# A binary cross-entropy over 8192 x 8192: seven small loads moved between the first large ones, and the last three stores dealt out anew

## The chip, the core and the metric

The kernel runs on one core of a Trainium2 chip. The metric is device time in microseconds (us), lower is better. The kernel before takes 1867.31 us as the median of three runs (1867.1 to 1867.54).

## The reference

Both inputs are 8192 x 8192 float32, 268 MB each, and so is the output.

```python
pred = np.clip(pred, eps, 1 - eps)          # eps = 1e-7
return -(target * np.log(pred) + (1 - target) * np.log(1 - pred))
```

`target` holds only 0 and 1, so every output element is the negative logarithm of either `pred` or `1 - pred`. Nothing is reduced: each element is read once from each input and written once.

## The kernel before, in words

The 67.1 million elements are laid over 128 partitions, 524,288 elements to each. `plan` cuts these into 37 chunks: two of 7680 columns (chunks 0 and 1), 32 of 15,360 columns (chunks 2 to 33), two of 7680 (chunks 34 and 35), and a last one of 2048 columns (chunk 36). All of it lives in two ring tiles, `ring_p` in float32 (the prediction, overwritten in place by every step up to the result) and `ring_t` in bfloat16 (the target, converted by the load itself). Each ring has two slots of 15,360 columns, which are used in turn, and a place of its own for chunk 36. A chunk of the small size takes half a slot.

One chunk goes through these steps. `load` brings target and prediction (L70, L71). `front_of` clips the prediction on VectorE (L100), adds `target - 1` on VectorE (L103), and takes the absolute value and the logarithm on ScalarE (L106, L107): |p + t - 1| is p where t is 1 and 1 - p where t is 0. `back_of` negates on VectorE (L110). `store` writes the result (L77). Large chunks are worked in two halves of 7680 columns, `(0, 2)` and `(1, 2)`.

The order on each engine is the order of the lines: the schedule is written by hand (`tc.manual_schedule`), and every engine issues its own instructions in that order and waits at each for what it needs. Nearly all DMAs are issued by GpSimd (POOL in the profile). SyncE (SP) issues only the prediction's load of chunk 0 and the stores of the last chunks, here chunks 34 and 35. A load into a slot waits for the store that empties the slot. Each of GpSimd's DMAs signals one of eight semaphores, taken in turn, and so it also waits for the DMA eight places before it on that engine to have landed. The DMA that an engine issues is split over 16 DMA engines, each of which works through its part of one queue in order.

Chunk 36 is loaded and stored in another layout (`mixed`, L81 to L83), and the prediction's part of it in uneven pieces, which the code calls teeth: a piece is 32 partitions by some multiple of 256 columns (`STEP`). One unit of 256 columns over 32 partitions is 32 KB, and the chunk has 32 units. The seven early pieces (`EARLY`, L93) have 8, 6, 4, 2, 6, 4 and 2 units; the eight late pieces (`LATE`, L97), which store the same chunk, have 8, 1, 4, 6, 6, 1, 2 and 4.

At the start the kernel before issues, on GpSimd, the target of chunk 0, target and prediction of chunk 1, target and prediction of chunk 2, and then four early pieces (L120 to L122). The other three early pieces follow the loads of chunk 3 (L132). In the main loop (L133 to L143) chunk k is worked and stored, and the chunk two places on is loaded. At the end (L144 to L158) z is chunk 33 and a and b are chunks 34 and 35: z is stored in two halves, a and b whole. On VectorE both halves of b's front come before the negation of a.

Of the kernel before, what the change touches and what calls it, by code (L numbers as in the profile page):

```python
# [1 line left out]

# [4 lines left out]

EPS = 1e-7

BIG = 15 * 1024  # L10
HALF = BIG // 2
STEP = 256
EARLY = ((0, 0, 8), (1, 0, 6), (2, 0, 4), (3, 0, 2), (3, 2, 8), (2, 4, 8), (1, 6, 8))
LATE = (
    (0, 0, 8), (1, 0, 1), (2, 0, 4), (3, 0, 6),
    (1, 2, 8), (1, 1, 2), (3, 6, 8), (2, 4, 8),
)


def plan(total):  # L20

    n, last = divmod(total, BIG)
    assert n > 4 and 0 < last <= 2048
    spots = [(HALF, 0), (HALF, HALF)]
    spots += [(BIG, k % 2 * BIG) for k in range(1, n - 1)]
    end = (n - 1) % 2 * BIG
    return spots + [(HALF, end), (HALF, end + HALF), (last, 2 * BIG)]

@with_exitstack
def kernel(
    ctx: ExitStack,
    tc: tile.TileContext,
    pred: bass.AP,
    target: bass.AP,
    out: bass.AP,
):
    nc = tc.nc
    fp32 = mybir.dt.float32  # L40
    bf16 = mybir.dt.bfloat16
    Alu = mybir.AluOpType
    Act = mybir.ActivationFunctionType
    P = nc.NUM_PARTITIONS

    R, C = pred.shape
    spots = plan(R * C // P)
    n = len(spots)
    widths = [w for w, _ in spots]
    cols = [sum(widths[:k]) for k in range(n)]  # L50

    def chunk(ap, k):
        flat = ap.rearrange("r c -> (r c)")
        end = R * C - cols[k] * P
        return flat[end - widths[k] * P : end].rearrange("(p w) -> p w", p=P)

    pool = ctx.enter_context(tc.tile_pool(name="rings", bufs=1))
    ring = [P, 2 * BIG + widths[-1]]
    ring_p = pool.tile(ring, fp32, name="ring_p", tag="ring_p")
    ring_t = pool.tile(ring, bf16, name="ring_t", tag="ring_t")  # L60
    warm = pool.tile([1, 8], fp32, name="warm", tag="warm")

    def spot(ring, k, part=(0, 1)):
        w, c = spots[k]
        i, m = part
        return ring[:, c + i * w // m : c + (i + 1) * w // m]

    def load(k):
        queue = nc.sync if k == 0 else nc.gpsimd
        nc.gpsimd.dma_start(out=spot(ring_t, k), in_=chunk(target, k))  # L70
        queue.dma_start(out=spot(ring_p, k), in_=chunk(pred, k))  # L71

    def store(k, part=(0, 1)):
        queue = nc.sync if k >= n - 3 else nc.gpsimd
        i, m = part
        w = widths[k] // m
        queue.dma_start(  # L77
            out=chunk(out, k)[:, i * w : (i + 1) * w], in_=spot(ring_p, k, part)
        )

    def mixed(ap):  # L81
        flat = ap.rearrange("r c -> (r c)")[: widths[-1] * P]
        return flat.rearrange("(b a w) -> a b w", b=8, a=16)  # L83

    def tooth_of(ap, j, lo, hi):
        return mixed(ap)[4 * j : 4 * j + 4, :, lo * STEP : hi * STEP]

    def tooth_in(j, lo, hi):
        return spot(ring_p, n - 1)[32 * j : 32 * j + 32, lo * STEP : hi * STEP]

    def load_teeth(teeth):
        for tooth in teeth:
            nc.gpsimd.dma_start(out=tooth_in(*tooth), in_=tooth_of(pred, *tooth))  # L93

    def store_teeth(teeth):
        for tooth in teeth:
            nc.gpsimd.dma_start(out=tooth_of(out, *tooth), in_=tooth_in(*tooth))  # L97

    def front_of(p, t):
        nc.vector.tensor_scalar(  # L100
            out=p, in0=p, scalar1=EPS, scalar2=1 - EPS, op0=Alu.max, op1=Alu.min
        )
        nc.vector.scalar_tensor_tensor(  # L103
            out=p, in0=t, scalar=1.0, in1=p, op0=Alu.subtract, op1=Alu.add
        )
        nc.scalar.activation(out=p, in_=p, func=Act.Abs)  # L106
        nc.scalar.activation(out=p, in_=p, func=Act.Ln)  # L107

    def back_of(p):
        nc.vector.tensor_scalar(out=p, in0=p, scalar1=-1.0, scalar2=None, op0=Alu.mult)  # L110

    def front(k, *part):
        front_of(spot(ring_p, k, *part), spot(ring_t, k, *part))

    def back(k, *part):
        back_of(spot(ring_p, k, *part))

    with tc.manual_schedule():
        nc.vector.memset(warm, 1.0)  # L119
        for k in range(3):  # L120
            load(k)
        load_teeth(EARLY[:4])  # L122
        nc.scalar.activation(out=warm, in_=warm, func=Act.Ln)  # L123
        front(0)
        front(1)
        back(0)
        store(0)
        back(1)
        store(1)
        load(3)  # L130
        nc.gpsimd.dma_start(out=spot(ring_t, n - 1), in_=mixed(target))  # L131
        load_teeth(EARLY[4:])  # L132
        for k in range(2, n - 4):  # L133
            front(k, (0, 2))
            front(k, (1, 2))
            back(k, (0, 2))
            back(k, (1, 2))
            store(k)
            for j in range(k + 2, n - 1 if k == n - 5 else k + 3):
                load(j)  # L140
            if k == 4:
                front(n - 1)
                back(n - 1)  # L143
        z, a, b = range(n - 4, n - 1)  # L144
        front(z, (0, 2))
        front(z, (1, 2))
        back(z, (0, 2))
        store(z, (0, 2))
        front(a)
        back(z, (1, 2))  # L150
        store(z, (1, 2))
        store_teeth(LATE)
        front(b, (0, 2))
        front(b, (1, 2))
        back(a)
        store(a)
        back(b)
        store(b)  # L158


# [1 line left out]
_INS = ['pred', 'target']  # L162
_OUTS = [((8192, 8192), 'float32')]


# [23 lines left out]
```

## Time and profile before

| | |
|---|---|
| median of three runs | 1867.31 us (1867.1 to 1867.54) |
| the profiled execution, its own time | 1866.22 us |
| its span in the trace | 1864.3 us |
| DMA engines, busy share in each fortieth of the span | 9 tenths or more |
| moved between HBM and the core | 536.87 MB read, 268.44 MB written |
| VectorE busy | 1122.4 us (60%) |
| ScalarE busy | 900.0 us (48%) |
| GpSimd busy | 68.6 us (4%) |

The span begins with the first instruction and ends with the last, and all points in time below count from its start. An engine's busy time leaves out its waits. A DMA is shown by the instruction that issues it and by the time from that to its landing, which is the moment when the last of the 16 DMA engines reports its part. The trace also keeps the report of each single DMA engine, so 16 landing times stand for each transfer; where the text says mean, first or last of the landings, these are meant. The loads of the target count with their bfloat16 size in the rate of the profile (GB/s), which is half of what they read.

### The profile page before, as it was taken

Reading aid. Unit: us, or ns where it says so; the run is one execution under the profiler, and the core shown is the slowest. Engines: PE = TensorE matmul, PEld = TensorE weight load, DVE = VectorE, ACT = ScalarE, POOL = GpSimd, SP = SyncE. Lnnn points to the kernel's source line nnn. Section 1 sums busy time; section 2 is a strip of 40 time slices with the busy share of each in tenths; the row PEclk is TensorE's granted clock in tenths of the full one; section 3 lists DMA queues with packets and bytes.
Section 4 is the critical chain, followed back from the end, with each engine's and each line's share of the span. In section 5 each row is a group of like instructions: output and inputs, shape, how many; then the busy total and the mean of one; then the engine's idle time right before and its main releaser. Section 6 shows DMA issues by size and latency. Waiting matters only on the chain.

```text
span 1864.3 us, 640 instructions
## 1 busy us (share of the span) xinstructions
DVE 1122.4 (60%) x210; ACT 900.0 (48%) x142; POOL 68.6 (4%) x126
## 2 busy tenths in 40 slices
DVE  4646676555666555566665556666555766555585
ACT  3345553345554334555433455543345554334555
POOL 1000000000000000000000000000000000000001
DMA  9999999999999999999999999999999999999999
GB/s 295 370 340 353 344 358 380 387 358 351 353 344 358 381 388 362 347 352 345 357 381 388 363 345 355 344 357 383 384 364 345 352 345 357 384 384 365 345 344 390
DMA packets 17620, 671.14 MB, mean 360 GB/s; under 512 B 3152, under 2 KB 3152, under 8 KB 3600
## 3 DMA queue, kind: packets, MB, share of 16 engines
q0 software_dynamic: 17184, 659.31, 98.7%
q1 hardware_dynamic: 432, 11.80, 1.5%
q14 instruction: 4, 0.03, 0.0%
HBM read 536.87 MB, written 268.44 MB: 432 GB/s over the span
## 4 chain that ended last, share of the span: by engine, by line
DMA 35%; issue 25%; ACT 23%; DVE 15%; POOL 1%; POOLq 0%; DVEq 0%; PEldq 0%
DMA ring_p<-in_pred_dram 32%; ACT ring_p L106 12%; ACT ring_p L107 11%; DVE ring_p L103 7%; DVE ring_p L100 4%; DVE ring_p L110 4%; DMA out_dram<-ring_p 3%; POOL ring_t L70 1%; POOL out_dram L77 0%; POOL ring_p L71 0%; POOLq L77 0%; DVEq L100 0%; POOLq L71 0%; PEldq L184 0%; POOLq L70 0%
## 5 line engine op out<-in xcount | busy, mean ns | idle before, releaser
L106 ACT ACTIVATE ring_p<-ring_p 128x7680 f32<-128x7680 f32 (+2 forms) x70 | 450.6, 6437 | 943.1 <-DVE ring_p L103 943.1
L103 DVE SCALAR_TENSOR_TENSOR ring_p<-ring_t,ring_p 128x7680 f32<-128x7680 bf16 (+2 forms) x70 | 557.2, 7960 | 2.4
L100 DVE TENSOR_SCALAR ring_p<-ring_p 128x7680 f32<-128x7680 f32 (+2 forms) x70 | 284.0, 4058 | 395.9 <-DMA ring_p<-in_pred_dram 395.9
L110 DVE TENSOR_SCALAR ring_p<-ring_p 128x7680 f32<-128x7680 f32 (+1 forms) x69 | 284.1, 4117 | 328.9 <-ACT ring_p L107 328.9
L107 ACT ACTIVATE ring_p<-ring_p 128x7680 f32<-128x7680 f32 (+2 forms) x70 | 451.1, 6444 | 2.2
L71 POOL DMA_DIRECT2D ring_p<-in_pred_dram x35 | 18.7, 534 | 921.7 <-DMA out_dram<-ring_p 921.7
L77 POOL DMA_DIRECT2D out_dram<-ring_p x35 | 19.8, 567 | 824.2 <-DVE ring_p L110 799.2
L70 POOL DMA_DIRECT2D ring_t<-in_target_dram x36 | 19.9, 552 | 1.1 <-PEq L184 0.8
L93 POOL DMA_DIRECT2D ring_p<-in_pred_dram x7 | 5.2, 762 | 16.3 <-DMA ring_t<-in_target_dram 16.3
L97 POOL DMA_DIRECT2D out_dram<-ring_p x8 | 4.7, 594 | 12.4 <-DMA out_dram<-ring_p 12.4
L123 ACT ACT_TABLE_LOAD x1 | 1.3, 1283 | 0.7 <-PEq L173 0.7
L131 POOL DMA_DIRECT2D ring_t<-in_target_dram x1 | 0.6, 557 | 0.0
L119 DVE MEMSET warm<- 1x8 f32 x1 | 0.1, 65 | 0.8 <-PEq L173 0.8
L123 ACT ACTIVATE warm<-warm 1x8 f32<-1x8 f32 x1 | 0.2, 207 | 0.0
L173 POOL MEMSET const-float32-0.0<- 128x1 f32 x1 | 0.1, 98 | 0.2 <-issue 0.2
L173 POOL MEMSET const-bfloat16-1.0<- 128x1 bf16 x1 | 0.1, 101 | 0.0
L173 POOL MEMSET const-float32-1.0<- 128x1 f32 x1 | 0.1, 98 | 0.0
L173 POOL MEMSET const-uint8-127<- 128x1 uint8 x1 | 0.1, 98 | 0.0
## 6 DMA issues: line engine op xcount, KB each, us to landing
ring_p<-in_pred_dram POOLq DMA_DIRECT2D x32, 7680.0 KB, 35.9
out_dram<-ring_p POOLq DMA_DIRECT2D x31, 7680.0 KB, 29.2
ring_t<-in_target_dram POOLq DMA_DIRECT2D x32, 3840.0 KB, 46.8
out_dram<-ring_p POOLq DMA_DIRECT2D x4, 3840.0 KB, 29.9
ring_p<-in_pred_dram POOLq DMA_DIRECT2D x3, 3840.0 KB, 35.0
ring_t<-in_target_dram POOLq DMA_DIRECT2D x4, 1920.0 KB, 27.7
out_dram<-ring_p SPq DMA_DIRECT2D x2, 3840.0 KB, 12.8
ring_p<-in_pred_dram SPq DMA_DIRECT2D x1, 3840.0 KB, 18.8
```

The costliest lines, as they stand in the source:

```text
L70: nc.gpsimd.dma_start(out=spot(ring_t, k), in_=chunk(target, k))
L71: queue.dma_start(out=spot(ring_p, k), in_=chunk(pred, k))
L77: queue.dma_start(out=chunk(out, k)[:, i * w : (i + 1) * w], in_=spot(ring_p, k, part))
L93: nc.gpsimd.dma_start(out=tooth_in(*tooth), in_=tooth_of(pred, *tooth))
L97: nc.gpsimd.dma_start(out=tooth_of(out, *tooth), in_=tooth_in(*tooth))
L100: nc.vector.tensor_scalar(out=p, in0=p, scalar1=EPS, scalar2=1 - EPS, op0=Alu.max, op1=Alu.min)
L103: nc.vector.scalar_tensor_tensor(out=p, in0=t, scalar=1.0, in1=p, op0=Alu.subtract, op1=Alu.add)
L106: nc.scalar.activation(out=p, in_=p, func=Act.Abs)
L107: nc.scalar.activation(out=p, in_=p, func=Act.Ln)
L110: nc.vector.tensor_scalar(out=p, in0=p, scalar1=-1.0, scalar2=None, op0=Alu.mult)
L123: nc.scalar.activation(out=warm, in_=warm, func=Act.Ln)
L131: nc.gpsimd.dma_start(out=spot(ring_t, n - 1), in_=mixed(target))
```

## The change

At the start, the order on GpSimd becomes: targets of chunks 0 and 1, four early pieces, prediction of chunk 1, target of chunk 2, the other three early pieces, prediction of chunk 2. (The prediction of chunk 0 stays on SyncE.) The three pieces behind the loads of chunk 3 are gone from there.

At the end, the second half of z's store goes to SyncE instead of GpSimd. The negation of a and its store come between the two halves of b's front. The negation and the store of b are done in two halves of 3840 columns.

```diff
+    def load_t(k):
+        nc.gpsimd.dma_start(out=spot(ring_t, k), in_=chunk(target, k))
+
+    def load_p(k):
+        queue = nc.sync if k == 0 else nc.gpsimd
+        queue.dma_start(out=spot(ring_p, k), in_=chunk(pred, k))
+
     def load(k):
-        queue = nc.sync if k == 0 else nc.gpsimd
-        nc.gpsimd.dma_start(out=spot(ring_t, k), in_=chunk(target, k))
-        queue.dma_start(out=spot(ring_p, k), in_=chunk(pred, k))
+        load_t(k)
+        load_p(k)
 
     def store(k, part=(0, 1)):
-        queue = nc.sync if k >= n - 3 else nc.gpsimd
         i, m = part
+        queue = nc.sync if k >= n - 3 or (k == n - 4 and i) else nc.gpsimd
...
         nc.vector.memset(warm, 1.0)
-        for k in range(3):
-            load(k)
+        load_p(0)
+        load_t(0)
+        load_t(1)
         load_teeth(EARLY[:4])
+        load_p(1)
+        load_t(2)
+        load_teeth(EARLY[4:])
+        load_p(2)
         nc.scalar.activation(out=warm, in_=warm, func=Act.Ln)
...
         nc.gpsimd.dma_start(out=spot(ring_t, n - 1), in_=mixed(target))
-        load_teeth(EARLY[4:])
...
         store_teeth(LATE)
         front(b, (0, 2))
-        front(b, (1, 2))
         back(a)
         store(a)
-        back(b)
-        store(b)
+        front(b, (1, 2))
+        back(b, (0, 2))
+        store(b, (0, 2))
+        back(b, (1, 2))
+        store(b, (1, 2))
```

## The prediction

> **What bounds the kernel now.** I read the page's slices and queues first, then the waits, then the timeline of the two ends.
>
> From the page, the slices and the traffic:
>
> ```profile
> DMA  9999999999999999999999999999999999999999
> GB/s 295 370 340 353 344 358 380 387 358 351 353 344 358 381 388 362 347 352 345 357 381 388 363 345 355 344 357 383 384 364 345 352 345 357 384 384 365 345 344 390
> HBM read 536.87 MB, written 268.44 MB: 432 GB/s over the span
> ```
>
> The DMA engines are busy from the first slice to the last. The rate swings because target loads are counted at half of what they read; by HBM traffic it is 432 GB/s over the whole span. The chain of work repeats this: the predictions of successive chunks are issued at 1680.37, 1734.73 and 1789.07, so a chunk takes 54.35 us for three transfers (target, prediction, result) that each have 7680 KB on the HBM side. That is 18.12 us for a transfer of 7680 KB and 9.06 us for one of 3840 KB. These two prices carry the rest.
>
> The waits say the same from the engines' side:
>
> ```profile
> ACT ring_p L106 <- DVE ring_p L103: 943.1, 36, 32.1
> POOL ring_p L71 <- DMA out_dram<-ring_p: 921.7, 32, 35.9
> DVE ring_p L100 <- DMA ring_p<-in_pred_dram: 395.9, 36, 18.7
> ```
>
> VectorE and ScalarE wait for data. GpSimd's long wait for a store to land looks like a stall and is none for the DMA engines: while prediction 3 waits until 98.55 for a slot, the target issued at 70.77 is still under way until 116.0 (45.3 us to landing).
>
> The time therefore is the DMA work of the slowest DMA engine plus whatever time it idles at the two ends. The timeline of the last 40 us:
>
> ```profile
> 1800.81 0.54 POOL L77 DMA_DIRECT2D out_dram<-ring_p  x1 [10.15 <-DVE ring_p L110]
> 1825.11 2.16 DVE L100 TENSOR_SCALAR ring_p<-ring_p 128x3840 f32<-128x3840 f32 x1 [1.65 <-DMA ring_p<-in_pred_dram]
> 1826.33 1.07 POOL L77 DMA_DIRECT2D out_dram<-ring_p  x1 [24.98 <-issue]
> 1827.39 3.53 POOL L97 DMA_DIRECT2D out_dram<-ring_p  x6
> 1837.65 4.15 DVE L110 TENSOR_SCALAR ring_p<-ring_p 128x7680 f32<-128x7680 f32 x1
> 1841.83 8.84 SPq L77 DMA_DIRECT2D out_dram<-ring_p  x2
> 1843.89 0.59 POOL L97 DMA_DIRECT2D out_dram<-ring_p  x1 [8.83 <-DMA out_dram<-ring_p]
> 1846.15 4.16 DVE L110 TENSOR_SCALAR ring_p<-ring_p 128x7680 f32<-128x7680 f32 x1 [4.35 <-ACT ring_p L107]
> ```
>
> And the stretches of 5 us, where the last two columns are the DMA share and the rate:
>
> ```profile
> 1830.00:1835.00 5.00, 4.97 (x3) 5.00 (x2) 1.46 (x3) 1.00 1.04 449
> 1835.00:1840.00 5.00, 5.00 (x2) 4.97 (x3) 0.06 (x1) 1.00 0.90 361
> 1840.00:1845.00 5.00, 1.80 (x1) 4.97 (x2) 0.59 (x1) 1.00 0.89 327
> 1845.00:1850.00 5.00, 3.85 (x1) 1.11 (x1) 0.00 (x0) 1.00 1.06 452
> ```
>
> There is the one visible hole: between 1835 and 1845 the rate is 361 and 327 against 432. The missing (71 + 105) GB/s over 5 us each are 0.88 MB, or 2.0 us of the 16 engines' work. What matters is whose it is.
>
> **Who idles at the end.** The landings, by issue plus time to landing, for the last engine: prediction of b 1825.1, first half of z 1834.2 (33.4 us after issue), second half of z 1843.6 (17.3), a 1854.3 (12.5), last late piece 1854.4 (10.5), b 1863.4 (13.1). Between prediction b and the end lie 38.3 us, of which four transfers of 9.06 are 36.2. The other 2.1 are pieces: 0.6 for the 2 of 32 units that fall to it (64 KB over four engines, at the same rate), and 1.5 for completions, since the landings of pieces on engines that get none of their data still come 0.18 apart, and there are eight. So the last engine has no idle time. The first engine is another matter: it reports the second late piece at 1838.89, the seventh at 1841.11 and a at 1852.29, which is 11.2 after the seventh, against 9.06 of work: it idled 2.1 us because a was issued only at 1841.83. The mean of the 16 landings shows 9.9 between them, 0.8 idle. At the end, the mean of the landings of b is 1862.42 and the last 1863.43. The hole is real, but it belongs to engines that finish early anyway.
>
> **The change, start.** Seven pieces, 1 MB, move from behind prediction 2 and behind prediction 3 to places between the first loads. The data are the same and so is the number of transfers, so the work of each DMA engine stays.
>
> - GpSimd's queue: targets 0 and 1, four pieces (about 0.6 us each to issue, from the four at L93), prediction 1, target 2 are eight issues, done by some 6.3 us. The ninth waits for the landing of the first, as before:
>
> ```profile
> 19.61 4.16 DVE L100 TENSOR_SCALAR ring_p<-ring_p 128x7680 f32<-128x7680 f32 x1 [18.75 <-DMA ring_p<-in_pred_dram]
> 22.14 1.75 POOL L93 DMA_DIRECT2D ring_p<-in_pred_dram  x1 [16.30 <-DMA ring_t<-in_target_dram]
> 40.11 4.16 DVE L100 TENSOR_SCALAR ring_p<-ring_p 128x7680 f32<-128x7680 f32 x1 [8.14 <-DMA ring_p<-in_pred_dram]
> 56.83 0.58 POOL L77 DMA_DIRECT2D out_dram<-ring_p  x1 [32.94 <-DVE ring_p L110]
> ```
>
> - So piece 5 goes at 22.1, piece 6 waits for target 1 (30.95), piece 7 for piece 1 and prediction 2 for piece 2. Pieces 1 and 2 land some 3.5 us after target 1 (pieces 1 to 4 took the last engine from 77.2 to 80.6 before), so prediction 2 is issued near 34.5. Target 2 keeps the engines at work until about 58 + 3, so 25 us remain before they would run dry.
> - Prediction 1 lands 2.4 to 3.5 us later than 40.1 (8 units on the busiest four engines, or those 3.5), so VectorE starts chunk 1 near 43 and the stores of chunks 0 and 1 go near 60 and 73 instead of 56.8 and 70.2. Prediction 2 lands near 81 instead of 77.2. In the queue stands work up to there, so both stores still come 8 us or more before their turn. Target 3 covers the slot's wait of prediction 3 for 18 us, as before. All these delays lie beside DMA work: cost nothing, and 3 us or so if one of these covers was gone.
> - What is unknown is what a piece costs beyond its bytes. By the means of the landings, target 2 to store 0 took 30.3 us, of which 28.7 are bytes: 1.6 too much for four pieces. Target 3 to the store of chunk 2 took 39.9, of which 39.6 are bytes (36.2, plus 3.3 for the target of chunk 36 and three pieces): 0.3 too much. Seven pieces at the cheap price are 0.8, at the dear one 2.8, against 1.9 now: from -1.1 to +0.9. The new places are like the old ones, amid full queues. I take 0.
>
> **The change, end.**
>
> - Second half of z on SyncE: its negation ends at 1823.45 (1819.30 + 4.15). SyncE issued a 0.03 after the negation's end (1837.65 + 4.15, then 1841.83), so this store goes at 1823.5 instead of 1826.33. The pieces, no longer behind it on GpSimd, go right after z's first half at 1801.35; pieces 5 to 7 then wait for the loads eight places back (1807, 1816, 1825), piece 8 for z's first half. So two queues run side by side from about 1824.5, z's second half against the rest of z's first half and the pieces. The work is the same. In one queue a completion of 0.18 us stands alone; beside another queue with data it may be covered. For the last engine that is between 0 and the 1.5 of above, plus 0.3 by which its second half of z took over 9.06. I take -0.7, under the middle, since only some of the eight fall beside other data.
> - [...] No row of this profile has small transfers on two queues.
> - Order of a: ScalarE ends a at 1832.57, VectorE ends the first half of b's sum at 1831.47. So the negation runs 1832.7 to 1836.9 and a is issued at 1837 instead of 1841.83. That closes the hole of the early engines (2.1 us). For the last engine it is worth 0, which had work until 1845.4 by its landings.
> - b's second half now waits on VectorE behind that negation: clip 1836.9 (was 1831.38), sum until 1843.3, ScalarE until 1850.1 (two passes of 3.4), second negation 2.16, last store issued at 1852.4 instead of 1850.34, the first half at 1845.4. On an idle engine issue to landing is 10.46 for 9.06 of data (a on the first engine), so 1.4 of lead is enough. The queue before the last half reaches to 1863.4 - 4.5 = 1858.9 on the last engine and about 1855.5 on the first: lead 5 and 1.7. It is covered; without that cover each us of lateness would cost a us.
> - One more transfer: between 0 (a to b are 9.1 on the last engine, the price of the bytes) and 1.4 (that lead, if it stood open). It is queued behind other data, hence nearest to the first: +0.1.
>
> Sum: 0 - 0.7 + 0.1 = -0.6. The profiled execution took 1866.22 with a span of 1864.3; the median is 1.09 above it. So 1865.6 for such an execution, and **1866.7** as the median.
>
> [...]
>
> **The rivals.**
>
> *The hole counts in full.* If the early engines take load off the late ones (shared paths), the 2.0 us of the hole and the spread of 1.0 between mean and last landing are worth having: -3.0, 1864.3. For it: the last engine took 9.4 where 9.06 was due just in that stretch. Against: the parts are dealt out to engines at issue, and the same late pieces go to the same engines. Chance 0.10.
>
> *Dear completions.* The pieces cost the dear price at the start (+0.9) and the split shows (+1.4 at most): up to 1869.6, half of it 1868.5. For it: 1.6 for the first four pieces. Chance 0.12.
>
> *Slower: b's data come late.* From 1824.5 z's second half on SyncE's queue competes with prediction b, which lands at 1825.1. If SyncE's queue went first, prediction b would land up to 9.06 later, the last store would go at 1861.5 and end 5.9 later at 1867.4, 4.0 over 1863.4: 1871.3. It decides once the last issue comes after 1857.5, that is, prediction b over 5 us late. Against: at 1824.5 nearly all of prediction b has moved, and chunk 0, where both queues load at once, shows both landing within 2.3 us (19.6 and 21.9). Chance 0.04.
>
> **How the numbers follow.** Forecast 0.74 (own range 1865.6 to 1867.6), hole in full 0.10, dear 0.12, late b 0.04. About 0.2%, or 3.7 us, is what a measurement tells from no change: faster means below 1863.6, slower above 1871.0. The hole in full stays above the first, with a third of its 0.10 below for what is not seen: faster 0.03. Slower 0.05: late b and a tail of the dear case. Same 0.92. The range for 8 in 10 reaches from the hole in full to the middle of the dear case: 1864.3 to 1868.5.
>
> **What would show it.** Right: prediction 2 issued near 34.5 and landing near 81, DMA share 9 in all slices; the late pieces issued from 1801; a issued near 1837; no dip to 361 and 327 after 1835; last landing between 1862 and 1863.5. Wrong: prediction b landing after 1826, the last store issued later than 1853, a new dip near 1855, or a chunk's cycle other than 54.35.

## The result, and the profile after

The changed kernel takes 1870.00 us (median of 22 runs, 1869.59 to 1870.33) against 1867.25 us (22 runs, 1866.77 to 1867.88) before: 2.75 us or 0.15% slower, ratio 1.0015 with a 95% interval of 1.0008 to 1.0021. Forecast were 1866.7 us and a range of 1864.3 to 1868.5; the time lies outside. The move stays within the 0.2% that the forecast called "same", but its sign is clear of the scatter and it is the wrong one.

The slices and the traffic in the page of the changed kernel:

```profile
span 1868.2 us, 643 instructions
DMA  9999999999999999999999999999999999999999
GB/s 290 347 339 347 351 365 383 384 349 353 353 346 362 385 382 359 345 353 354 351 387 385 356 354 346 351 357 380 387 361 349 353 347 354 383 383 366 350 344 381
HBM read 536.87 MB, written 268.44 MB: 431 GB/s over the span
```

Nothing has changed in kind: the DMA engines are busy in every slice, and the same bytes take longer. Only the second slice stands out, with 347 GB/s where it was 370 (47 to 93 us).

The timeline of its start (start us, length us, engine, line, instruction, and in brackets the idle time before and what ended it):

```profile
22.34 1.74 POOL L99 DMA_DIRECT2D ring_p<-in_pred_dram  x1 [16.34 <-DMA ring_t<-in_target_dram]
35.94 0.59 POOL L73 DMA_DIRECT2D ring_p<-in_pred_dram  x1
44.16 4.16 DVE L106 TENSOR_SCALAR ring_p<-ring_p 128x7680 f32<-128x7680 f32 x1 [12.01 <-DMA ring_p<-in_pred_dram]
60.88 0.56 POOL L83 DMA_DIRECT2D out_dram<-ring_p  x1 [24.35 <-DVE ring_p L116]
84.47 4.16 DVE L106 TENSOR_SCALAR ring_p<-ring_p 128x7680 f32<-128x7680 f32 x1 [10.49 <-DMA ring_p<-in_pred_dram]
```

Prediction 2 is issued at 35.94 (forecast 34.5) and store 0 at 60.88 (forecast 60), but VectorE gets prediction 2 at 84.47, where 81 was forecast. Before, VectorE got it at

```profile
77.18 4.16 DVE L100 TENSOR_SCALAR ring_p<-ring_p 128x7680 f32<-128x7680 f32 x1 [7.25 <-DMA ring_p<-in_pred_dram]
```

The end:

```profile
1826.42 29.05 SPq L83 DMA_DIRECT2D out_dram<-ring_p  x4
1828.05 2.16 DVE L106 TENSOR_SCALAR ring_p<-ring_p 128x3840 f32<-128x3840 f32 x1 [1.66 <-DMA ring_p<-in_pred_dram]
1835.63 4.16 DVE L116 TENSOR_SCALAR ring_p<-ring_p 128x7680 f32<-128x7680 f32 x1 [1.23 <-ACT ring_p L113]
1845.33 0.59 POOL L103 DMA_DIRECT2D out_dram<-ring_p  x1 [15.01 <-DMA out_dram<-ring_p]
1852.95 2.16 DVE L116 TENSOR_SCALAR ring_p<-ring_p 128x3840 f32<-128x3840 f32 x1 [4.83 <-ACT ring_p L113]
```

and its stretches of 5 us (DMA share and GB/s are the last two columns):

```profile
1833.00:1838.00 5.00, 3.77 (x2) 5.00 (x2) 0.00 (x0) 1.00 0.98 422
1838.00:1843.00 5.00, 4.96 (x3) 4.29 (x2) 0.00 (x0) 1.00 0.95 401
1843.00:1848.00 5.00, 5.00 (x2) 1.92 (x1) 0.59 (x1) 1.00 1.05 429
1853.00:1858.00 5.00, 2.11 (x1) 0.00 (x0) 0.00 (x0) 1.00 1.00 400
1858.00:1863.00 5.00, 0.00 (x0) 0.00 (x0) 0.00 (x0) 1.00 0.99 396
```

On VectorE the order at the end came out as worked out, some 3 us later throughout: prediction b arrives at 1828.05 instead of 1825.11, and a's negation, behind the front of b's first half, starts at 1835.63, where 1832.7 was forecast. On the queues it did not. The first half of z lands at 1845.05, 41.3 us after its issue (33.4 before), now that z's second half runs beside it on SyncE's queue, and the eighth late piece waits for that landing until 1845.33. The hole of 361 and 327 GB/s is gone, but from 1853 to 1863 the rate is 400 and 396. Nothing was gained.

The landings divide the loss. The mean landing of the store of chunk 4 (all pieces are in by then) is 263.51 before and 266.68 after: +3.17. From there to the mean landing of prediction b both take the same, 1558.16 and 1558.10. From the last landing of prediction b to the last landing of all it is 38.35 before and 38.77 after: +0.42. The profiled executions differ by 3.8 (1866.22 and 1869.99), more than the medians do, because the one of before was 1.0 below its own median.

### The profile page after: what moved, and what is told of

It reads as the page before. It is cut to its first block, busy times and chain, and to the rows that moved or that the text cites. A ratio compares the mean times of both kernels' runs of the same rounds, so it can differ in the third digit from the quotient of the medians.

```text
span 1868.2 us, 643 instructions
## 1 busy us (share of the span) xinstructions
DVE 1122.5 (60%) x211; ACT 900.1 (48%) x142; POOL 72.5 (4%) x125
## 4 chain that ended last, share of the span: by engine, by line
DMA 35%; issue 26%; ACT 22%; DVE 15%; POOL 1%; POOLq 0%; DVEq 0%; PEldq 0%
DMA ring_p<-in_pred_dram 32%; ACT ring_p L113 11%; ACT ring_p L112 11%; DVE ring_p L109 7%; DVE ring_p L116 4%; DVE ring_p L106 4%; DMA out_dram<-ring_p 3%; POOL ring_t L69 0%; POOL out_dram L83 0%; POOL ring_p L73 0%; POOL ring_p L99 0%; POOLq L83 0%; DVEq L106 0%; PEldq L196 0%; POOLq L69 0%
## 5 line engine op out<-in xcount | busy, mean ns | idle before, releaser
L106 DVE TENSOR_SCALAR ring_p<-ring_p 128x7680 f32<-128x7680 f32 (+2 forms) x70 | 284.0, 4057 | 398.8 <-DMA ring_p<-in_pred_dram 398.8
L116 DVE TENSOR_SCALAR ring_p<-ring_p 128x7680 f32<-128x7680 f32 (+2 forms) x70 | 284.2, 4060 | 330.6 <-ACT ring_p L113 330.6
L83 POOL DMA_DIRECT2D out_dram<-ring_p x34 | 18.7, 550 | 797.5 <-DVE ring_p L116 797.5
L103 POOL DMA_DIRECT2D out_dram<-ring_p x8 | 9.7, 1212 | 32.0 <-DMA out_dram<-ring_p 15.0
```

Of the source, the lines that this page charges most:

```text
L83: queue.dma_start(out=chunk(out, k)[:, i * w : (i + 1) * w], in_=spot(ring_p, k, part))
L106: nc.vector.tensor_scalar(out=p, in0=p, scalar1=EPS, scalar2=1 - EPS, op0=Alu.max, op1=Alu.min)
```

## The experiments

Each kernel is the one before or the changed one with a few lines altered. In "excess" below, a group is pieces 1 to 4 or pieces 5 to 7; the excess is the mean landing of the large transfer behind the group, minus the mean landing of the large transfer ahead of it, minus the bytes of both the group and that transfer behind it at 9.06 us for 3840 KB (1.51 and 0.91 for the two groups). Prediction 2, which has a load ahead of it and no piece between, took 0.4 to 0.5 more than its bytes before and in the kernel without pieces (the last one below), so differences of that size are not read as the pieces' own unless they repeat.

### Start and end apart

One kernel has the edits at the end alone:

```diff
-        queue = nc.sync if k >= n - 3 else nc.gpsimd
+        queue = nc.sync if k >= n - 3 or (k == n - 4 and i) else nc.gpsimd
...
         front(b, (0, 2))
-        front(b, (1, 2))
         back(a)
         store(a)
-        back(b)
-        store(b)
+        front(b, (1, 2))
+        back(b, (0, 2))
+        store(b, (0, 2))
+        back(b, (1, 2))
+        store(b, (1, 2))
```

and one the edit at the start alone:

```diff
-        for k in range(3):
-            load(k)
+        load_p(0)
+        load_t(0)
+        load_t(1)
         load_teeth(EARLY[:4])
+        load_p(1)
+        load_t(2)
+        load_teeth(EARLY[4:])
+        load_p(2)
...
-        load_teeth(EARLY[4:])
```

> The kernel before with the three edits at the end alone. Theory H (the loss lies at the start, because a piece costs more than its bytes where a large load follows it): 1867.2 to 1868.0 us, that is 0 to +0.8 against before; prediction b still lands 38 to 39 us before the last landing. Theory E (the loss lies at the end, because the late pieces crawl beside large stores on another queue): 1869.0 to 1870.3.

> The kernel before with the edit at the start alone. Theory H: 1869.3 to 1870.3 us (+2 to +3), and the main loop runs 2.5 to 3.5 us later than before from its first chunk on. Theory E: 1867.0 to 1867.6, the loop at most 0.5 later.

The end alone took 1867.82 us against 1867.28 (ratio 1.0004, 0.9995 to 1.0013), the start alone 1869.70 (1.0013, 1.0004 to 1.0022). Both times lie where theory H had them: nearly all of the loss lies at the start, and the 0.5 of the end alone is within its interval. In the traces it is plainer than in the times: the store of chunk 4 lands at 263.50 with the edits at the end and at 266.60 with the edit at the start (before 263.51, changed 266.68). The lag is then carried through 1500 us of main loop; the load that waits for the last large store is issued, in the kernel with the edits at the end,

```profile
1788.65 0.53 POOL L71 DMA_DIRECT2D ring_p<-in_pred_dram  x1 [28.41 <-DMA out_dram<-ring_p]
```

and in the kernel with the edit at the start

```profile
1791.64 0.53 POOL L73 DMA_DIRECT2D ring_p<-in_pred_dram  x1 [28.40 <-DMA out_dram<-ring_p]
```

### All early pieces behind prediction 2

```diff
         for k in range(3):
             load(k)
-        load_teeth(EARLY[:4])
+        load_teeth(EARLY)
...
-        load_teeth(EARLY[4:])
```

> The kernel before with all seven early pieces behind the prediction of chunk 2, so that a store follows them in the queue and no load. Theory H: 1866.8 to 1867.9 us, since the same pieces with the same unevenness cost little before a store. Rival S (the unevenness costs because it comes before the first stores, whatever follows): 1869 to 1870, since the uneven start is nearly as early as in the changed kernel.

It took 1873.7 us (1.0035, 1.0022 to 1.0048), worse than either theory said, and for a reason of its own. The waits on GpSimd in the first 100 us hold

```profile
POOL out_dram L77 <- DMA ring_p<-in_pred_dram: 18.5, 1, 18.5
```

and the timeline

```profile
77.23 4.26 POOL L77 DMA_DIRECT2D out_dram<-ring_p  x2 [18.46 <-DMA ring_p<-in_pred_dram]
```

with these stretches (DMA share and GB/s last):

```profile
75.00:80.00 5.00, 3.36 (x1) 0.00 (x0) 2.77 (x1) 1.00 0.79 168
80.00:85.00 5.00, 4.97 (x2) 0.00 (x0) 2.01 (x3) 1.00 0.83 338
```

In the traces of before and after GpSimd's DMAs name semaphores 99 to 106 in turn, and from the ninth on each goes only after the one eight places before it has landed, 0.28 us later at the soonest. Store 0 stands eight places behind prediction 2 here, with the seven pieces between them: ready at 56, it waited for prediction 2 to land and went at 77.23; the DMA share fell to 0.79 and the engines ran dry. By the store of chunk 4, which lands at 268.15, this start is 4.6 behind the kernel before, where the prediction gave 3 or so for a cover that is gone. Another 3 us are lost at the end, which is taken up below. On the question it was made for the run says nothing.

### The same pieces, other partitions

```diff
-EARLY = ((0, 0, 8), (1, 0, 6), (2, 0, 4), (3, 0, 2), (3, 2, 8), (2, 4, 8), (1, 6, 8))
+EARLY = ((2, 0, 8), (3, 0, 6), (0, 0, 4), (1, 0, 2), (1, 2, 8), (0, 4, 8), (3, 6, 8))
```

(with `LATE` exchanged in the same way, on the edit at the start alone)

> [...] Theory P (a piece slows the DMA engine that normally serves the partitions it writes, so it matters which partitions it writes while a load runs): the excess over the bytes moves by at least 0.5 us between pieces 1 to 4 and pieces 5 to 7, and the time by 0.5 to 2 us against the edit at the start alone. Without P (order alone decides): each excess and the time within 0.4 us of that of the edit at the start alone.

Time 1869.37 us (1.0011, 1.0002 to 1.0020). The excess of the first group went from 2.01 to 3.12, that of the second from 2.52 to 1.51, as theory P had it; their sum stayed at 4.5 to 4.6. The time moved by 0.3, where theory P had 0.5 at least. So it matters which partitions a piece writes, with sizes, order and places equal.

### Each group ahead of a store

```diff
-        load_teeth(EARLY[:4])
...
         nc.gpsimd.dma_start(out=spot(ring_t, n - 1), in_=mixed(target))
-        load_teeth(EARLY[4:])
+        load_teeth(EARLY[:4])
...
+            if k == 2:
+                load_teeth(EARLY[4:])
```

> The kernel before with no piece among the first loads: pieces 1 to 4 behind the target of chunk 36 and pieces 5 to 7 behind the loads of chunk 4, each group followed by a store in the queue, with free places among the eight DMAs in flight. Theory L (a piece disturbs a load that follows it, since both write the partitions, and not a store that follows it): the excess over the bytes is at most 0.6 us in each group by the mean landings, and the time 1865.8 to 1867.3 us. Without L (a piece costs the same anywhere): excess 1.5 or more in the first group, and the time 1867 to 1869.

Time 1866.99 us against 1867.05 (0.9999, 0.9990 to 1.0009). The excess is 1.16 and 0.19: the second group as theory L has it, the first above its 0.6 and below the 1.5 of the other side. Beside the 2.01 and 2.52 of the same pieces ahead of a load, that is 0.85 and 2.3 less. The groups also stand later in the queue here, so this run alone does not part the store behind them from the place; the kernels below do, which change the partitions and keep the places.

### Row by row, and over all partitions

In one kernel, on the edit at the start alone, chunk 36 is laid out row by row like the other chunks, and the pieces keep their 32 partitions. The layout was made so that no DMA engine should get more than another; whether that came about, no run shows.

```diff
-        return flat.rearrange("(b a w) -> a b w", b=8, a=16)
+        return flat.rearrange("(p w) -> p w", p=P)
...
-        return mixed(ap)[4 * j : 4 * j + 4, :, lo * STEP : hi * STEP]
+        return mixed(ap)[32 * j : 32 * j + 32, lo * STEP : hi * STEP]
```

> [...] Theory P (what costs is that a DMA engine writes partitions which another one serves, while a load runs): the pieces and the load behind them still take at least 1 us over their bytes in each group. Rival U (what costs is that some DMA engines get more than others): the excess in each group falls under 0.6 us, and the main loop starts 2 us earlier than with the edit at the start alone.

In the other the pieces have, besides, all 128 partitions and a quarter of the columns (`EARLY`, `LATE` and `tooth_of` change to match). They were cut so that each DMA engine should write the same partitions as in the large transfers; whether it does, no run shows.

```diff
-STEP = 256
+STEP = 64
...
-        return spot(ring_p, n - 1)[32 * j : 32 * j + 32, lo * STEP : hi * STEP]
+        return spot(ring_p, n - 1)[:, lo * STEP : hi * STEP]
...
```

> [...] Sizes, number and places of the pieces stay. Theory P: the pieces and the load behind them take at most 0.8 us over their bytes in the first group and 0.6 in the second (completions only), and the main loop starts at least 2.5 us earlier than with the edit at the start alone. Rival R (short rows are what costs): excess of 1 us or more in each group, since the rows are four times shorter than before. [...]

Row by row, with 32 partitions: excess 1.42 and 0.85. The expectation had either 1 or more in each or under 0.6 in each; neither theory got it. The store of chunk 4 lands at 264.89, 1.7 earlier than with the edit at the start alone, but the time is 1870.57 us (1.0014, 1.0006 to 1.0023), no better than its 1869.70; why is open. All the excess was in the pieces (2.89 us for 1.51 of bytes, 1.74 for 0.91), nearly twice their price; the loads behind them took 9.10 and 18.13, the price of their bytes.

Over all partitions: excess 1.05 and 0.21 (0.8 and 0.6 at most were expected), and the store of chunk 4 lands at 263.95, 2.65 earlier than with the edit at the start alone, in the same places of the queue and with rows four times shorter. Time 1866.57 us against 1867.27 (0.9998, 0.9989 to 1.0007). Here VectorE gets prediction 2 at

```profile
80.22 4.16 DVE L106 TENSOR_SCALAR ring_p<-ring_p 128x7680 f32<-128x7680 f32 x1 [7.44 <-DMA ring_p<-in_pred_dram]
```

instead of 84.47 in the changed kernel, close to the 81 of the forecast. The new places cost no more than the old ones by themselves; the 32-partition pieces in them do.

### Uneven pieces, `OWN` and `OTHER`

```diff
+OWN = ((0, 8), (1, 6), (4, 4), (5, 2))
+OTHER = ((4, 8), (5, 6), (0, 4), (1, 2))
...
+        return flat.rearrange("(b a w) -> a b w", b=4, a=32)
...
+        for j, u in teeth:
+            nc.gpsimd.dma_start(
+                out=spot(ring_p, n - 1)[16 * j : 16 * j + 16, : u * STEP],
+                in_=mixed(pred)[4 * j : 4 * j + 4, :, : u * STEP],
+            )
...
         load_t(1)
-        load_teeth(EARLY[:4])
+        load_teeth(OWN)
         load_p(1)
         load_t(2)
-        load_teeth(EARLY[4:])
+        load_teeth(OTHER)
         load_p(2)
...
```

This is the edit at the start alone with other pieces. Each group has four pieces of 16 partitions with 8, 6, 4 and 2 KB a row, in this order. `OWN` writes partitions 0 to 15, 16 to 31, 64 to 79 and 80 to 95, `OTHER` 64 to 79, 80 to 95, 0 to 15 and 16 to 31. The names are the author's: a piece of `OWN` was meant to be written by DMA engines that write its partitions in the large transfers too, a piece of `OTHER` by different ones. No trace shows which DMA engine writes which partitions, so theory P's forecasts for the two groups rest on an assumption.

> [...] The whole prediction of chunk 36 is loaded once more behind chunk 3, so the total time holds 1 MB more and says nothing; the start alone is read. Theory P: the first group and prediction 1 take at most 0.9 us over their bytes, the second group and prediction 2 at least 0.7 us more than that. Rival U (unevenness alone costs): both within 0.4 us of each other.

> The same with the two groups exchanged, so that the place of a group tells nothing by itself. Theory P: now the first group and prediction 1 take at least 0.7 us more over their bytes than the first group of the run before, and the second group and prediction 2 at least 0.7 us less than its second group. Rival U: each within 0.4 us of the run before.

A group is 0.75 us of bytes here. By the mean landings, in one execution of each kernel:

| order | first group and prediction 1: excess | second group and prediction 2: excess |
|---|---|---|
| `OWN`, then `OTHER` | 0.19 | 1.22 |
| `OTHER`, then `OWN` | 0.95 | 0.17 |

In either place `OWN` costs 0.17 to 0.19 over its bytes and `OTHER` 0.95 to 1.22. VectorE sees prediction 1 in the first kernel (`OWN` ahead of it) at

```profile
40.91 4.16 DVE L110 TENSOR_SCALAR ring_p<-ring_p 128x7680 f32<-128x7680 f32 x1 [8.99 <-DMA ring_p<-in_pred_dram]
```

and in the second (`OTHER` ahead of it) at

```profile
41.74 4.16 DVE L110 TENSOR_SCALAR ring_p<-ring_p 128x7680 f32<-128x7680 f32 x1 [9.92 <-DMA ring_p<-in_pred_dram]
```

Theory P's numbers hold in both kernels: the three differences for which it needed 0.7 are 1.03, 0.76 and 1.05. The sizes (128, 96, 64 and 32 KB) are the same in all four groups and do not explain them.

### The end in parts

Each of the two edits at the end was also made alone: the order (a's negation between b's halves, b in halves) without the first two lines of the diff above,

```diff
         front(b, (0, 2))
-        front(b, (1, 2))
         back(a)
         store(a)
+        front(b, (1, 2))
...
```

and the move of z's second half without the rest:

```diff
-        queue = nc.sync if k >= n - 3 else nc.gpsimd
+        queue = nc.sync if k >= n - 3 or (k == n - 4 and i) else nc.gpsimd
```

> Of the edits at the end only the order (negation and store of a between the halves of b, b negated and stored in halves); the second half of z stays on GpSimd ahead of the late pieces. Theory C (late pieces crawl, packet by packet, beside large stores on another queue, and then end after b): the pieces land earlier than with all edits at the end, b ends last, and the time is 1866.3 to 1867.4. Without C: as with all edits at the end, 1867.8 within 0.5.

> Of the edits at the end only the move of the second half of z's store to SyncE's queue; a and b as before. Theory C: the first late pieces land within 2 us of that store and some of them only with a, the seventh later than 1846, but b is issued and lands as before; the time is 1867.0 to 1868.0. If the crawl costs nothing: 1866.4 to 1867.0, since the hole before a shrinks.

The order alone took 1867.90 us against 1867.05 (1.0003, 0.9995 to 1.0012), the move alone 1866.94 (1.0000, 0.9991 to 1.0009). Neither can be told from the kernel before. From the last landing of prediction b to the last of all it is 39.11 and 38.63, with all edits at the end 38.73, in the changed kernel 38.77; with the old end it is 38.35 (before) and 38.76 to 39.48 in seven kernels with edits at the start. An eighth, with all early pieces behind prediction 2, took 41.52. That one apart, new or old, the end takes the same, within the 1.1 us by which these single executions differ.

The crawl of theory C is there. In the changed kernel the fifth late piece (issued at 1810.16) and the eighth (1845.33) show, each in its own window:

```profile
out_dram<-ring_p POOLq DMA_DIRECT2D x1, 192.0 KB, 56.1
```

```profile
out_dram<-ring_p POOLq DMA_DIRECT2D x1, 128.0 KB, 21.5
```

For the eighth piece the kernel before has

```profile
out_dram<-ring_p POOLq DMA_DIRECT2D x1, 128.0 KB, 10.5
```

Much of the 56.1 is a wait for the first half of z, which stands ahead in the same queue until 1845.05; in the other 21 us nothing but pieces is left in that queue. The last of all landings, 1866.8, is that of the eighth piece, and b's last half had landed at 1865.9. With z's second half alone on SyncE's queue the seventh piece landed at 1845.8, with no crawl; with the order alone, the last seven pieces landed between 1856 and 1863.8, around b's 1863.7. So it is a, issued on the other queue while pieces are still to go, that they crawl beside. The kernel with the end of 41.52 agrees: it has the old order, but a was issued at 1846.62 with four pieces still to come, and these landed between 1856 and 1871.4. What the crawl costs is not shown: the times of the order alone and of the move alone fell where their expectations had it costing nothing, and the order alone was not faster than all edits at the end, as theory C would have it.

### The late pieces in the loop, and no pieces at all

```diff
+            if k in (8, 10):
+                store_teeth(LATE[:4] if k == 8 else LATE[4:])
...
-        store_teeth(LATE)
```

> All edits at the end, the start as before, and the late pieces stored in the main loop (four behind the loads of chunk 10, four behind those of chunk 12) instead of at the end. Theory C (the late pieces' crawl beside large stores is what eats the gain of the edits at the end): b's last half ends last, the hole before a is gone, and the time is 1865.8 to 1867.0 us, below all edits at the end with the pieces there (1867.82). Without C: 1867.4 to 1868.4.

```diff
-        load_teeth(EARLY[:4])
...
-        nc.gpsimd.dma_start(out=spot(ring_t, n - 1), in_=mixed(target))
-        load_teeth(EARLY[4:])
+        load(n - 1)
...
                 back(n - 1)
+                store(n - 1)
...
-        store_teeth(LATE)
```

> All edits at the end, and chunk 36 treated like any other chunk: one load of target and one of prediction behind the loads of chunk 3, one store in the main loop. There are no pieces at all and 13 transfers fewer. If pieces cost what the means of the landings say (completions of 0.18 us for each and an excess of 1.3 us in the kernel before), this gives 1863.8 to 1866.0 us, below both kernels. If the pieces earn their cost by holding the DMA engines apart: 1867 or more.

Both have all edits at the end, and both end in 36.35 us after prediction b, which is four transfers of 9.06 and nothing else. With the pieces in the loop, the stretches where the hole was read

```profile
1835.00:1840.00 5.00, 3.79 (x2) 5.00 (x2) 0.00 (x0) 1.00 1.01 436
1840.00:1845.00 5.00, 4.96 (x3) 3.46 (x2) 0.00 (x0) 1.00 1.03 442
```

So the new order leaves the end no idle time, once no small transfers are in its way; whether the old order would leave any without them was not tried. The late pieces' share of the end, 38.35 less 36.35, is 2.0, close to the 2.1 that the prediction gave them. But the first took 1868.39 us against 1867.27 (1.0008, 0.9999 to 1.0017), above the 1867.0 of theory C and at the edge of the other range: from the store of chunk 4 to prediction b it needs 1562.97 instead of 1558.1, 4.9 more, of which the 1 MB is 2.4. Of the other 2.5 only 0.3 and 0.4 lie at the two groups themselves; the rest comes in the chunks between and behind them (55.1 us for the first instead of 54.35), and its cause was not pursued. The second took 1866.61 us (0.9996, 0.9987 to 1.0005), between its two expectations. Neither it nor the one with pieces over all partitions can be told from the kernel before.

## Why the prediction was wrong

**The bound and the prices held.** DMA work in the queue's order sets the time (none of GpSimd's 122 DMAs before lands ahead of the one issued before it); 1558.1 us of main loop are the same in both kernels, and in the two kernels without late pieces at the end the halves of the last store, with nothing beside them, land 4.56 and 4.55 after what stands ahead of them, where half of 9.06 is 4.53. On GpSimd's queue, prediction b of the kernel before lands 9.09 after target b, against 9.06 of bytes.

**The queue at the start held.** Issues came within 1.5 us of the forecast and the engines did not run dry. In the one run in which they did, the start lost 4.6.

**The step that failed** is the price of a piece beyond its bytes: "from -1.1 to +0.9. The new places are like the old ones, amid full queues. I take 0." It is +3.2. The excess:

| kernel | pieces 1 to 4 | pieces 5 to 7 | sum |
|---|---|---|---|
| before (a store behind each group) | 1.17 | 0.20 | 1.37 |
| changed (a load behind each group) | 2.14 | 2.47 | 4.61 |
| edit at the start alone | 2.01 | 2.52 | 4.53 |
| the same, partitions exchanged | 3.12 | 1.51 | 4.63 |
| each group ahead of a store | 1.16 | 0.19 | 1.35 |
| changed places, pieces over all partitions | 1.05 | 0.21 | 1.26 |

The difference of the sums of the first two rows is 3.2, which is the lag of the main loop (3.17). The places are not alike: the old ones have a store behind them, which reads the partitions, the new ones a load, which writes them. It is shown that what follows a piece decides, and which partitions it writes (rows 2 to 6, and the two kernels with `OWN` and `OTHER`, where a group of four costs 0.2 beyond its bytes as `OWN` and 0.95 to 1.22 as `OTHER`). The 1.1 or so that the first group costs even ahead of a store or over all partitions is unexplained; `OWN` in the same place (0.19) does not have it. By its landings a piece of 32 partitions is moved by four DMA engines (of the first one's 16 landings in the changed kernel, twelve come by 31.7 and four from 34.5 on). An account that would fit is theory P: these four write partitions that in the load behind belong to other DMA engines, and both are slowed while that load runs. It is argued and not shown: no trace shows which DMA engine writes which partitions, nor how a slowing would come about, and `OWN` and `OTHER` rest on the author's assumption. Why the pieces laid out row by row took 2.89 and 1.74 us for 1.51 and 0.91 of bytes is not shown either.

Both prices that the prediction had, 1.6 and 0.3, came from groups with a store behind them, so no range between them could hold for a place ahead of a load; that the new places have a load behind them was in view before the change. The 1.6 also contained 0.4 of prediction 2 itself.

**The end.** That the hole belongs to engines which finish early and is worth 0 for the last one agrees with the runs: it is closed and the end takes as long, though the crawl came with the same edit. The -0.7 for completions covered by a second queue did not show: the ends with z's second half beside the pieces take 38.6 to 38.8, those without it 38.35 to 39.5. The split at +0.1 was right, as the halves above tell. So two terms failed: the start, +3.2 instead of 0, and the completions, nothing to be seen instead of -0.7. The forecast also worked out no delay for z's first half beside the second queue; it landed 41.3 us after its issue instead of 33.4, and the late piece that waited for it landed last of all.

**The rivals.** The hole in full did not come. Engines that are ahead take nothing over from those behind in the profile before: first and last of the 16 landings stay 5.02 to 5.10 us apart in all 53 transfers that land from 448 to 1390 us. Prediction b was not held up: it lands 1558.1 after chunk 4's store as before, so the slower rival was no part of it. The dear completions had the sign and the place, but their 0.9 at the start was capped by the dearest price seen in a place with a store behind it.

## What to carry to other kernels

A group of small loads of 32 partitions cost 0.2 to 1.2 us over its bytes ahead of a store here, and 0.85 to 3.1 ahead of a load (0.85 where chunk 36 was laid out row by row); over all 128 partitions it cost 0.2 to 1.1 ahead of a load. So put such loads ahead of a store, or give them all the partitions. A price read in some places of the profile holds for a new one only if what stands behind it there is of the same kind. Closing a hole in the rate of all DMA engines together gained nothing here, where the last engine had no part in it by its own landings; look at those first.

## What the runs showed that was not expected

- Small transfers on one queue were held up by large ones on another: beside the stores of a and b the eighth late piece, 128 KB, landed 21.5 us after its issue instead of 10.5.
- That GpSimd's DMAs wait for the one eight places before cost time: with seven small ones in a row a ready store went 21 us late (77.23 for 56), and the start lost 4.6.
- DMA engines that started in step did not stay so. With no pieces at all the 16 landings of a transfer lie 0.7 us apart at 77 us, 2.6 at 360 and 3.9 at 1645; while they were within 3 us, a chunk took about 0.1 us more than its 54.35. Whether holding the engines apart is what the uneven pieces are good for was not tried.
